# Layer 0's expert products in tiles 32 columns wide, and a written order for the step into layer 1

## The chip, the cores and the metric

The kernel runs as one program on one core of a Trainium2 chip. The metric is the time of one execution on the device in microseconds (us); lower is better. Three runs of the kernel before gave 1434.01, 1437.96 and 1445.67 us, median 1437.96 us. All inputs and outputs are float32.

## The reference, cut to what matters

Two layers work on 256 latent tokens x and 256 context tokens ctx, 1024 features each. Each layer is a mixer, then a mixture of experts. The part of the reference that the change touches is layer 0's mixture and the way into layer 1:

```python
def hier_moe(h, wg, bg, we, be, w1, w3, w2):
    ...                                # top-1 group of 4, top-2 expert in it, weights in combine
    for e in range(16):
        y = (jax.nn.silu(h @ w1[e]) * (h @ w3[e])) @ w2[e]     # 1024 -> 512 -> 1024
        out = out + combine[:, e:e + 1] * y
...
xc = xc + g2_c * y[256:]               # layer 0: context and latent tokens
xl = xl + g2_x * y[:256]
...
hx = modulate(xl, norm_g[1, 0], sh1_x, sc1_x)      # layer 1 begins: RMSNorm, scale, shift
hc = modulate(xc, norm_g[1, 0], sh1_c, sc1_c)
p = hx @ od_w_in, hc @ od_w_in                     # query columns 0:512 are needed of hx alone
```

So layer 1's first projection needs every expert's result for the x tokens, and the same for ctx a little later.

## The kernel before, in words

**Layer 0's experts** (`all0`). Each expert gets up to 96 tokens, gathered by an indirect DMA into `xe` and transposed to `XE` (features on partitions, 96 tokens). The tokens are the stationary operand of TensorE and the weights stream past. 96 does not fit two or four times into 128 columns, so the tokens are cut: 64 of them go into bank A (`h`, slice `ab`), two products side by side (w1 and w3), and 32 into bank C (`hc`, slice `cc`), four products side by side (w1 and w3, two slices of the features each). `hidden(e, q)` does that for a quarter q of the features: four A products, then four C products. In float32 each product is two matmul instructions. `middle(e)` puts A and C together, applies silu and the product (ScalarE, then VectorE), four transposes make `gT`, and `down(e, gT)` multiplies by w2, again 64 tokens wide into `y[0]` and 32 wide into `y[1]`, in two halves of the hidden features. Experts 14 and 15 go through `down` 96 wide instead, and their sums into the tokens are made by TensorE (`last_two`).

The order on an engine is written out where instructions are stamped: `in_line` stamps every matmul and transpose, `put` and `token[0]` stamp ScalarE and VectorE instructions with the name "moe"; stamped instructions of an engine stay in program order. All others are placed by a planner that has its own costs and due times. In loop e the order of TensorE is: hidden(e+1, 0), transposes of gT, hidden(e+1, 1), down(e), transposes of tokens (`xt`), hidden(e+1, 2), transposes, hidden(e+1, 3).

**Weights** come as units of 512 KB through SyncE's DMA queue into a ring of 30 slots, which is cut to 10 after expert 11 (`without(late)`). A slot is filled again when TensorE has used it.

**The step into layer 1.** Experts 0 to 13 write their results to DRAM; 8 indirect DMAs bring them back by token (`room`), and `fetched(n)` adds two of them to 128 tokens: one ScalarE and three VectorE instructions (L940 to L943), n = 0 to 3, the x tokens first. `last_two(a, t)` adds experts 14 and 15: four matmuls into a bank of tag `h` for each half of the features, then two VectorE instructions (L1083, L1084). `norm1_begin` and `norm1_end` norm the x tokens between these. Then `proj1` loads layer 1's first weights (L202), `split` cuts each into a high and a low part (ScalarE `whi`, VectorE `wlo`, both at L224), and `norm1_turn` transposes the x tokens and splits them too. The matmuls of `proj1` (`pj`) also write to banks of tag `h`, of which there are three. None of the weights' splits and transposes here is stamped. The ctx tokens are normed and transposed during the first projection.

Of the kernel before, what the change touches and what calls it, by code (L numbers as in the profile page):

```python
# [135 lines left out]
def tile_kernel(ctx: ExitStack, tc: tile.TileContext, I, out, stage=99, dbg=None):  # L136
# [81 lines left out]
    def flip(*args):  # L218
        inst = nc.tensor.transpose(*args)  # L219
        if in_line[0]:  # L220
            inorder(inst, "line")
# [124 lines left out]
    def norm1_begin(x, t, put):  # L346

        i, n = 1 if t < 2 else 0, token_tile(norm1["xn"], t)
        for h in range(2):
            hs = slice(h * 512, h * 512 + 512)  # L350
            put(act(n[:, hs], token_tile(x, t)[:, hs], AF.Square, accum_out=norm1["st"][:, t, h:h + 1]))
            put(V.tensor_tensor(n[:, hs], token_tile(x, t)[:, hs], norm1["sc"][i][:, hs], op=ALU.mult))

    def norm1_end(t, put):

        i, n, st = 1 if t < 2 else 0, token_tile(norm1["xn"], t), norm1["st"]
        s = st[:, t, 0:1]
        put(V.tensor_tensor(s, s, st[:, t, 1:2], op=ALU.add))
        put(V.tensor_scalar(s, s, 1.0 / D, 1e-6, op0=ALU.mult, op1=ALU.add))
        put(act(s, s, AF.Sqrt))  # L360
        put(V.reciprocal(s, s))
        for g in range(2):
            hs = slice(g * 512, g * 512 + 512)
            put(V.scalar_tensor_tensor(n[:, hs], n[:, hs], s, norm1["sh"][i][:, hs], op0=ALU.mult, op1=ALU.add))

    def norm1_turn(x, khi, klo):

        xn = norm1["xn"]
        xn[0] = cp.tile([P, 2, D], F32, tag="x4", name="xn")
        for t in (2, 3, 0, 1):  # L370
            c = slice(t * 128, t * 128 + 128)
            if t < 2:
                norm1_begin(x, t, lambda inst: None)
                norm1_end(t, lambda inst: None)
            for g in range(2):
                tp = ps("nT", ("ga", "gT")[g])
                for k in range(4):
                    flip(tp[:, k * 128:(k + 1) * 128], token_tile(xn, t)[:, (4 * g + k) * 128:(4 * g + k + 1) * 128],
                         ident)
                split(tp.rearrange("p (k t) -> p k t", k=4), khi[g][:, :, c], klo[g][:, :, c])  # L380
            if t == 3:
                yield xn
        yield

    def split_tiles():

# [63 lines left out]
    def moe(l, tiles, cap, ng, x1, pm, pn, hhi=None, hlo=None):  # L450
# [182 lines left out]
        def experts(pe, ysb, rest, spare=None, next_norm=None):  # L633
# [178 lines left out]
            def all0(rest):  # L812
# [61 lines left out]
                def hidden(e, q):  # L874


                    if q == 0:
                        hs[e] = ps("h", "h"), ps("hc", "h")
                    w = [weights(e, u) for u in (ups[q][1], ups[q][0])]
                    A, C = hs[e]  # L880
                    for i in range(2):
                        for j in range(2):
                            mm(A[64 * j:64 * j + 64, :], XTe[e][:, 2 * q + i, ab], w[j][:, i], start=(q + i == 0),
                               stop=(q + i == 4))
                    for i in range(2):
                        for j in range(2):
                            r0 = 64 * i + 32 * j
                            mm(C[r0:r0 + 32, :], XTe[e][:, 2 * q + i, cc], w[j][:, i], start=(q == 0), stop=(q == 3))
# [22 lines left out]
                def down(e, gT):  # L911


                    y = [ps("y", "y") for _ in range(2)]
                    if e > 13:
                        for f in range(4):
                            w = weights(e, 8 + f)
                            for h in range(2):
                                mm(y[h][r], gT[:, f], w[:, h], start=(f == 0), stop=(f == 3))
                        return y  # L920
                    for g in range(2):
                        ws = [weights(e, 8 + 2 * g + i) for i in range(2)]
                        for i in range(2):
                            for h in range(2):
                                mm(y[0][64 * h:64 * h + 64, :], gT[:, 2 * g + i, ab], ws[i][:, h], start=(g + i == 0),
                                   stop=(g + i == 2))
                        for i in range(2):
                            for h in range(2):
                                r0 = 64 * i + 32 * h
                                mm(y[1][r0:r0 + 32, :], gT[:, 2 * g + i, cc], ws[i][:, h], start=(g == 0), stop=(g == 1))  # L930
                    return y
# [66 lines left out]
                for e in range(16):  # L998
# [9 lines left out]
                    if e < 15:  # L1008
                        hidden(e + 1, 1)
                    else:  # L1010
                        for n in (2, 3):
                            fetched(n, put)
                    y = down(e, gT)
                    if e < 14:
                        o = ysb[:, e % 2, :]
# [48 lines left out]
                                    out=rooms[2 * n_ + i], out_offset=None, in_=yD,  # L1064
                                    in_offset=bass.IndirectOffsetOnAxis(ap=idx[:, i, a:a + 1], axis=0))
                in_line[0] = False
                token[0] = None
                slots[:] = base
                turn[0] = 0
                yhi, ylo, PT = last["yhi"], last["ylo"], last["PT"]  # L1070
                warm(AF.Sqrt, yhi(1, 1)[r])
                sums = pe.tile([P, 2, D], F32, tag="rm0", name="tt")

                def last_two(a, t):

                    for h in range(2):
                        acc = ps("sc", "h")
                        for i in range(2):
                            mm(acc, PT[r, i, a], yhi(i, h)[r], start=(i == 0), stop=False)
                            mm(acc, PT[r, i, a], ylo(i, h)[r], start=False, stop=(i == 1))  # L1080
                        hs_ = slice(h * 512, h * 512 + 512)
                        tt = sums[:, a % 2, hs_]
                        put(V.tensor_tensor(tt, acc, g2[t][:, hs_], op=ALU.mult))  # L1083
                        put(V.tensor_tensor(token_tile(x1, t)[:, hs_], tt, token_tile(x1, t)[:, hs_], op=ALU.add))  # L1084


                begin1, end1 = next_norm[1:]
                last_two(*order[0])
                begin1(x1, 2, put)
                last_two(*order[1])  # L1090
                end1(2, put)
                begin1(x1, 3, put)
                end1(3, put)
                for n in (2, 3):
                    last_two(*order[n])

            def all1():

# [684 lines left out]
    with tc.tile_pool(name="pe0", bufs=1) as pe:  # L1783
        ysb = pP.tile([P, 2, D], F32, tag="vT", name="ysb")

        def spare():
            a = [pe.tile([P, 2, 512], F32R, name=f"yhi{i}") for i in range(2)]
            b = pP.tile([P, 4, 512], F32R, tag="y", name="spare")
            c = pe.tile([P, 2, 512], F32R, name="PT0")
            return (lambda i, h: a[i][:, h]), (lambda i, h: b[:, 2 * i + h]), c.rearrange("p i (a t) -> p i a t", a=4)  # L1790

        experts(pe, ysb, rest, spare, (norm1_scales, norm1_begin, norm1_end))
    es_m.close()
    if "x2" in dbg:
        for i in range(2):
# [31 lines left out]
    with ExitStack() as es:  # L1827
# [1 line left out]
        dqT = xtile([4, 256])  # L1829
        dkT = [xtile([2, 512]) for _ in range(2)]  # L1830
        dv = pP.tile([P, 4, 512], F32, tag="y", name="dv")
        kt = [[pP.tile([P, 4, 512], F32R, tag=t, name=t) for t in tags] for tags in (("rT", "kT"), ("vT", "kkn"))]
        khi, klo = ([t[k // 4][:, k % 4, :] for k in range(8)] for t in kt)
        norm = norm1_turn(x1, *kt)
        with tc.high_priority(offset=150):
            xn = next(norm)
        c1 = pA.tile([P, NC1], F32, name="c1")
        nc.scalar.dma_start(c1, I["cst1"])
        def proj1(c0, n, evac):

            for i in range(4):
                if i % 2 == 0:
                    ws = [wload(Wd[h * 512:(h + 1) * 512, c0 + i * 128:c0 + i * 128 + 256], 4, 256)
                          for h in range(2)]
                whi, wlo = (t.rearrange("p a (k f) -> p (a k) f", f=128) for t in split_tiles())
                for h in range(2):
                    split(ws[h][:, :, (i % 2) * 128:(i % 2 + 1) * 128], whi[:, 4 * h:4 * h + 4, :],
                          wlo[:, 4 * h:4 * h + 4, :])
                acc = ps("pj", "pj")
                for k in range(8):  # L1850
                    mm(acc[:, 0:n], whi[:, k, :], khi[k][:, 512 - n:], start=(k == 0), stop=False)
                    mm(acc[:, 0:n], whi[:, k, :], klo[k][:, 512 - n:], start=False, stop=False)
                    mm(acc[:, 0:n], wlo[:, k, :], khi[k][:, 512 - n:], start=False, stop=(k == 7))
                evac(i, acc)
# [26 lines left out]
        def ev_dq(i, acc):  # L1881
            act(dqT[:, i, :], acc[:, 0:256], AF.Copy)
            rope(dqT[:, i, :])
            if i == 1:
                next(norm)

        def ev_dk(i, acc):
            act(dkT[i // 2][:, i % 2, :], acc, AF.Copy)
# [163 lines left out]
```

## Time and profile before

| | |
|---|---|
| median of three runs | 1437.96 us (1434.01 to 1445.67) |
| the profiled execution | 1443.12 us, its span 1441.1 us |
| mean granted TensorE clock over the span | 0.930 |
| busy: PE, DVE, ACT, POOL | 1267.0, 590.1, 425.6, 218.1 us |
| bytes moved by DMA | 349.22 MB, mean 242 GB/s |

PE is TensorE's matmuls, PEld its weight loads, DVE VectorE, ACT ScalarE, POOL GpSimd, SP SyncE. A matmul's end is modelled, so the distance between starts says more than a duration. Times on the left of a row are us from the start of the span. In brackets stands how long the engine was idle ahead of the row, and what ended that.

### The profile page before, as it was taken

What the parts mean: (1) busy time and instruction counts of PE and PEld (TensorE: products, weight loads), DVE (VectorE), ACT (ScalarE), POOL (GpSimd) and SP (SyncE); (2) the same over time, 40 slices, a digit from 0 to 9 for tenths busy, and PEclk for the clock granted to TensorE, in tenths of its full rate; (3) what the DMA queues carried; (4) which work ended last, traced back from release to release, by engine and by line L of the source; (5) the groups of instructions that cost most, each with busy time, mean ns of one, the idle gap of its engine ahead of it and who ended that gap; (6) DMA issues with size and microseconds to landing.
All of it is one profiled execution on the core that took longest, in us unless ns stands there. A gap on an engine that the chain in (4) does not pass through costs nothing. (4 is left out here: it accounts for less than half of the span.)

```text
span 1441.1 us, 22145 instructions
## 1 busy us (share of the span) xinstructions
PE 1267.0 (88%) x8700; PEld 687.0 (48%) x8700; DVE 590.1 (41%) x1329; ACT 425.6 (30%) x835; POOL 218.1 (15%) x271
## 2 busy tenths in 40 slices
PE   5999778888989886999999987799998699999975
PEld 0556556666756672222222223776766544433321
DVE  1326846778656632222112238744636611110003
ACT  2753322222223321221222123324637321111102
POOL 0005520333411301111111120310000100000000
PEclk9999989989999967999999996799999799999998
DMA  9687677766783757999998790651442679999554
GB/s 335 209 256 216 179 181 203 174 172 177 183 262 129 248 221 275 369 383 383 380 382 304 256 365 23 147 139 59 146 169 88 208 265 398 400 396 395 222 223 172
DMA packets 240320, 349.22 MB, mean 242 GB/s; under 512 B 96120, under 2 KB 126104, under 8 KB 239952
## 3 DMA queue, kind: packets, MB, share of 16 engines
q1 hardware_dynamic: 226240, 304.72, 62.9%
q0 software_dynamic: 11264, 34.72, 7.4%
q10 hardware_dynamic: 2704, 8.27, 1.6%
q8 instruction: 72, 1.18, 0.3%
q14 instruction: 40, 0.33, 0.1%
HBM read 326.86 MB, written 20.79 MB: 241 GB/s over the span
## 5 line engine op out<-in xcount | busy, mean ns | idle before, releaser
L214 PE MATMUL y<-w,gT 128*64 128x512 f32 (+2 forms) x736 | 163.0, 612 | 2.1 <-ACT gT L698 1.5
L214 PE MATMUL pj<-hh,whi 128*128 128x512 f32 x432 | 150.1, 429 | 0.6 <-ACT hh L224 0.3
L214 PE MATMUL h<-w,XT 128*64 128x512 f32 x512 | 138.6, 614 | 5.1 <-issue 5.1
L224 DVE TENSOR_TENSOR wlo<-w,whi 128x512 fp32r<-128x512 f32 (+1 forms) x104 | 84.7, 828 | 111.5 <-ACT whi L224 107.4
L214 PE MATMUL h<-w,XE 128*64 128x512 f32 x512 | 125.4, 611 | 3.0 <-ACT XE L790 2.5
L224 ACT ACTIVATE whi<-w 128x512 fp32r<-128x512 f32 (+1 forms) x104 | 69.9, 700 | 155.4 <-DMA w<-in_ev_w_in_dram 73.0
L214 PEld LDWEIGHTS pj<-hh,whi 128*128 128x128 f32 x432 | 83.6, 202 | 32.4 <-issue 9.8
L214 PEld LDWEIGHTS y<-w,gT 128*64 128x64 f32 (+2 forms) x736 | 44.9, 131 | 101.7 <-issue 91.4
L214 PE MATMUL pj<-hh,wlo 128*128 128x512 f32 x216 | 89.9, 418 | 2.1 <-DVE wlo L224 2.0
L214 PE MATMUL ada<-w,sT 128*32 128x512 f32 x384 | 69.0, 639 | 16.9 <-DMA w<-in_ada_w_dram 10.0
L214 PE MATMUL hc<-w,XE 128*32 128x512 f32 x512 | 68.2, 605 | 0.1
L214 PEld LDWEIGHTS h<-w,XT 128*64 128x64 f32 x512 | 36.4, 138 | 63.6 <-issue 57.6
L894 DVE TENSOR_TENSOR ysb<-y,ysb 64x512 f32<-64x512 f32 x14 | 9.7, 695 | 139.1 <-ACT ysb L893 139.1
L214 PEld LDWEIGHTS h<-w,XE 128*64 128x64 f32 x512 | 31.3, 137 | 57.1 <-issue 48.1
L806 DVE SCALAR_TENSOR_TENSOR ylo<-y,sw,yhi 128x512 fp32r<-128x512 f32 x16 | 12.0, 751 | 100.7 <-ACT yhi L805 100.7
L214 PEld LDWEIGHTS pj<-hh,wlo 128*128 128x128 f32 x216 | 43.5, 201 | 17.0 <-DVE wlo L224 4.7
L689 DVE TENSOR_TENSOR gg<-gg,h 64x512 f32<-64x512 f32 x16 | 11.1, 691 | 95.0 <-ACT gg L688 95.0
L2024 POOL TENSOR_TENSOR x<-x,fg 128x512 f32<-128x512 f32 x2 | 2.8, 1378 | 284.9 <-ACT sq L2023 284.9
L1020 POOL DMA_DIRECT2D yD<-ysb x28 | 15.1, 545 | 171.7 <-ACT ysb L1016 171.7
L1016 ACT ACTIVATE ysb<-y 128x512 f32<-128x512 f32 x14 | 8.4, 597 | 99.6 <-PE y L214 99.6
L1316 DVE TENSOR_TENSOR pr<-T,X 128x8 f32<-128x8 f32 (+14 forms) x120 | 35.7, 298 | 4.0 <-DMA X<-xs 0.6
L893 ACT ACTIVATE gs<-hc 64x512 f32<-64x512 f32 x16 | 9.4, 588 | 88.7 <-PE hc L214 88.7
(542 smaller groups left out, 2269.1 us busy)
## 6 DMA issues: line engine op xcount, KB each, us to landing
w<-in_moe_w_dram SPq DMA_DIRECT2D x384, 512.0 KB
w<-in_ada_w_dram SPq DMA_DIRECT2D x96, 512.0 KB
w<-in_ev_w_in_dram SPq DMA_DIRECT2D x27, 512.0 KB
w<-in_od_w_in_dram SPq DMA_DIRECT2D x24, 512.0 KB
sD<-wad SPq DMA_DIRECT2D x16, 256.0 KB
w<-in_ev_w_out_dram SPq DMA_DIRECT2D x8, 512.0 KB
w<-in_od_w_out_dram SPq DMA_DIRECT2D x8, 512.0 KB
yD<-ysb POOLq DMA_DIRECT2D x28, 128.0 KB, 5.3
```

Source lines behind the costliest of these rows:

```text
L214: inst = nc.tensor.matmul(*args, **kw)
L224: for inst in (act(hi, src, AF.Copy), V.tensor_tensor(lo, src, hi.bitcast(F32), op=ALU.subtract)):
L689: V.tensor_tensor(gg[64:128], gg[64:128], acc[64:128], op=ALU.mult)
L806: V.scalar_tensor_tensor(lo, y, w, hi.bitcast(F32), op0=ALU.mult, op1=ALU.subtract))
L893: put(act(o, acc[0:64, :], AF.Copy))
L894: put(V.tensor_tensor(o, acc[64:128, :], o, op=ALU.add))
L1016: put(act(o[:, 0:512], y[0], AF.Copy))
L1020: nc.gpsimd.dma_start(yD[e * cap:e * cap + 64, hs_], o[64 * h:64 * h + 64, 0:512])
L1316: V.tensor_tensor(pr[:, :, 0:t], T[:, 0:t, :].rearrange("p s j -> p j s"), X[:, 0:t, t][:, None, :].to_broadcast([P, 8, t]), op=ALU.mult)
L2024: (V if h else G).tensor_tensor(xt_[:, hs], xt_[:, hs], fg[:, hs], op=ALU.mult)
```

## The change

Three things. In `hidden` and `down` each product of 64 tokens becomes two of 32 (tokens 0:32 and 32:64), so that all these products have 32 columns and four stand side by side; bank C, `y[1]` and experts 14 and 15 in `down` stay as they were. Layer 1's first two weight loads (columns 0:256) are written in expert 15's loop after gT's copy, and their two splits get a stamped place: the first after `fetched(3)` and ahead of `down(15)`, the second after the x tokens' transposes. The x tokens' transposes and splits are stamped too, each right behind the norm of its 128 tokens, and the ctx sums of `last_two` come last, into banks of the tags `y` and `ps` in place of `h`.

```diff
@@ -363,24 +363,41 @@
             hs = slice(g * 512, g * 512 + 512)
             put(V.scalar_tensor_tensor(n[:, hs], n[:, hs], s, norm1["sh"][i][:, hs], op0=ALU.mult, op1=ALU.add))
 
-    def norm1_turn(x, khi, klo):
-
-        xn = norm1["xn"]
-        xn[0] = cp.tile([P, 2, D], F32, tag="x4", name="xn")
-        for t in (2, 3, 0, 1):
-            c = slice(t * 128, t * 128 + 128)
-            if t < 2:
-                norm1_begin(x, t, lambda inst: None)
-                norm1_end(t, lambda inst: None)
-            for g in range(2):
-                tp = ps("nT", ("ga", "gT")[g])
-                for k in range(4):
-                    flip(tp[:, k * 128:(k + 1) * 128], token_tile(xn, t)[:, (4 * g + k) * 128:(4 * g + k + 1) * 128],
-                         ident)
-                split(tp.rearrange("p (k t) -> p k t", k=4), khi[g][:, :, c], klo[g][:, :, c])
-            if t == 3:
-                yield xn
-        yield
+    def norm1_turn(t):
+
+        if not norm1.get("kt"):
+            norm1["kt"] = [[pP.tile([P, 4, 512], F32R, tag=tg, name=tg) for tg in tags]
+                           for tags in (("rT", "kT"), ("vT", "kkn"))]
+        khi, klo = norm1["kt"]
+        c = slice(t * 128, t * 128 + 128)
+        for g in range(2):
+            tp = ps("nT", ("ga", "gT")[g])
+            for k in range(4):
+                flip(tp[:, k * 128:(k + 1) * 128],
+                     token_tile(norm1["xn"], t)[:, (4 * g + k) * 128:(4 * g + k + 1) * 128], ident)
+            split(tp.rearrange("p (k t) -> p k t", k=4), khi[g][:, :, c], klo[g][:, :, c])
+
+    def norm1_ctx(x):
+
+        norm1["xn"][0] = cp.tile([P, 2, D], F32, tag="x4", name="xn")
+        for t in range(2):
+            norm1_begin(x, t, lambda inst: None)
+            norm1_end(t, lambda inst: None)
+            norm1_turn(t)
+
+    first_w = {}
+
+    def first_weights():
+
+        Wq = I["od_w_in"][0]
+        ws = [wload(Wq[h * 512:(h + 1) * 512, 0:256], 4, 256) for h in range(2)]
+
+        def make(i):
+            whi, wlo = first_w[i] = [t.rearrange("p a (k f) -> p (a k) f", f=128) for t in split_tiles()]
+            for h in range(2):
+                split(ws[h][:, :, i * 128:(i + 1) * 128], whi[:, 4 * h:4 * h + 4, :], wlo[:, 4 * h:4 * h + 4, :])
+
+        return make
 
     def split_tiles():
 
@@ -880,8 +897,9 @@
                     A, C = hs[e]
                     for i in range(2):
                         for j in range(2):
-                            mm(A[64 * j:64 * j + 64, :], XTe[e][:, 2 * q + i, ab], w[j][:, i], start=(q + i == 0),
-                               stop=(q + i == 4))
+                            for b in (0, 32):
+                                mm(A[64 * j + b:64 * j + b + 32, :], XTe[e][:, 2 * q + i, b:b + 32], w[j][:, i],
+                                   start=(q + i == 0), stop=(q + i == 4))
                     for i in range(2):
                         for j in range(2):
                             r0 = 64 * i + 32 * j
@@ -922,8 +940,9 @@
                         ws = [weights(e, 8 + 2 * g + i) for i in range(2)]
                         for i in range(2):
                             for h in range(2):
-                                mm(y[0][64 * h:64 * h + 64, :], gT[:, 2 * g + i, ab], ws[i][:, h], start=(g + i == 0),
-                                   stop=(g + i == 2))
+                                for b in (0, 32):
+                                    mm(y[0][64 * h + b:64 * h + b + 32, :], gT[:, 2 * g + i, b:b + 32], ws[i][:, h],
+                                       start=(g + i == 0), stop=(g + i == 2))
                         for i in range(2):
                             for h in range(2):
                                 r0 = 64 * i + 32 * h
@@ -1008,8 +1027,13 @@
                     if e < 15:
                         hidden(e + 1, 1)
                     else:
+                        load(len(stream))
+                        slots[:] = base
+                        turn[0] = 0
+                        first = next_norm[3]()
                         for n in (2, 3):
                             fetched(n, put)
+                        first(0)
                     y = down(e, gT)
                     if e < 14:
                         o = ysb[:, e % 2, :]
@@ -1064,17 +1088,14 @@
                                     out=rooms[2 * n_ + i], out_offset=None, in_=yD,
                                     in_offset=bass.IndirectOffsetOnAxis(ap=idx[:, i, a:a + 1], axis=0))
                 in_line[0] = False
-                token[0] = None
-                slots[:] = base
-                turn[0] = 0
                 yhi, ylo, PT = last["yhi"], last["ylo"], last["PT"]
                 warm(AF.Sqrt, yhi(1, 1)[r])
                 sums = pe.tile([P, 2, D], F32, tag="rm0", name="tt")
 
-                def last_two(a, t):
+                def last_two(a, t, banks):
 
                     for h in range(2):
-                        acc = ps("sc", "h")
+                        acc = ps("sc", banks[h])
                         for i in range(2):
                             mm(acc, PT[r, i, a], yhi(i, h)[r], start=(i == 0), stop=False)
                             mm(acc, PT[r, i, a], ylo(i, h)[r], start=False, stop=(i == 1))
@@ -1084,15 +1105,19 @@
                         put(V.tensor_tensor(token_tile(x1, t)[:, hs_], tt, token_tile(x1, t)[:, hs_], op=ALU.add))
 
 
-                begin1, end1 = next_norm[1:]
-                last_two(*order[0])
+                begin1, end1, _, turn1 = next_norm[1:]
+                last_two(*order[0], "hh")
                 begin1(x1, 2, put)
-                last_two(*order[1])
+                last_two(*order[1], ("h", "ps"))
                 end1(2, put)
+                turn1(2)
                 begin1(x1, 3, put)
                 end1(3, put)
-                for n in (2, 3):
-                    last_two(*order[n])
+                turn1(3)
+                first(1)
+                last_two(*order[2], "yy")
+                last_two(*order[3], ("ps", "y"))
+                token[0] = None
 
             def all1():
 
@@ -1789,7 +1814,7 @@
             c = pe.tile([P, 2, 512], F32R, name="PT0")
             return (lambda i, h: a[i][:, h]), (lambda i, h: b[:, 2 * i + h]), c.rearrange("p i (a t) -> p i a t", a=4)
 
-        experts(pe, ysb, rest, spare, (norm1_scales, norm1_begin, norm1_end))
+        experts(pe, ysb, rest, spare, (norm1_scales, norm1_begin, norm1_end, first_weights, norm1_turn))
     es_m.close()
     if "x2" in dbg:
         for i in range(2):
@@ -1829,23 +1854,23 @@
         dqT = xtile([4, 256])
         dkT = [xtile([2, 512]) for _ in range(2)]
         dv = pP.tile([P, 4, 512], F32, tag="y", name="dv")
-        kt = [[pP.tile([P, 4, 512], F32R, tag=t, name=t) for t in tags] for tags in (("rT", "kT"), ("vT", "kkn"))]
-        khi, klo = ([t[k // 4][:, k % 4, :] for k in range(8)] for t in kt)
-        norm = norm1_turn(x1, *kt)
-        with tc.high_priority(offset=150):
-            xn = next(norm)
+        khi, klo = ([t[k // 4][:, k % 4, :] for k in range(8)] for t in norm1["kt"])
+        xn = norm1["xn"]
         c1 = pA.tile([P, NC1], F32, name="c1")
         nc.scalar.dma_start(c1, I["cst1"])
         def proj1(c0, n, evac):
 
             for i in range(4):
-                if i % 2 == 0:
+                if i % 2 == 0 and (c0 or i):
                     ws = [wload(Wd[h * 512:(h + 1) * 512, c0 + i * 128:c0 + i * 128 + 256], 4, 256)
                           for h in range(2)]
-                whi, wlo = (t.rearrange("p a (k f) -> p (a k) f", f=128) for t in split_tiles())
-                for h in range(2):
-                    split(ws[h][:, :, (i % 2) * 128:(i % 2 + 1) * 128], whi[:, 4 * h:4 * h + 4, :],
-                          wlo[:, 4 * h:4 * h + 4, :])
+                if c0 or i > 1:
+                    whi, wlo = (t.rearrange("p a (k f) -> p (a k) f", f=128) for t in split_tiles())
+                    for h in range(2):
+                        split(ws[h][:, :, (i % 2) * 128:(i % 2 + 1) * 128], whi[:, 4 * h:4 * h + 4, :],
+                              wlo[:, 4 * h:4 * h + 4, :])
+                else:
+                    whi, wlo = first_w[i]
                 acc = ps("pj", "pj")
                 for k in range(8):
                     mm(acc[:, 0:n], whi[:, k, :], khi[k][:, 512 - n:], start=(k == 0), stop=False)
@@ -1882,7 +1907,7 @@
             act(dqT[:, i, :], acc[:, 0:256], AF.Copy)
             rope(dqT[:, i, :])
             if i == 1:
-                next(norm)
+                norm1_ctx(x1)
 
         def ev_dk(i, acc):
             act(dkT[i // 2][:, i % 2, :], acc, AF.Copy)
```

## Rows read from the trace of the kernel before

**Rows 1.** Stretches: us, busy us of each engine (instructions), granted clock, DMA share, GB/s.
```profile
368.00:376.00 8.00, 8.00 (x124) 5.99 (x123) 2.13 (x11) 0.98 (x2) 5.61 (x5) 1.00 0.58 119
600.00:640.00 40.00, 40.00 (x248) 11.20 (x244) 8.91 (x16) 8.37 (x15) 6.04 (x10) 1.00 1.04 382
867.00:870.00 3.00, 2.14 (x5) 1.18 (x6) 2.77 (x4) 0.63 (x1) 0.00 (x0) 0.50 0.04 11
```

**Rows 2.** Timeline, 640 to 652 us: start, length, engine, line, operation, tiles, count.
```profile
643.80 0.55 PE L219 MATMUL xt<-cst,xe 96*128 96x96 f32 x4
...
646.15 1.07 PE L214 MATMUL hc<-w,XE 128*32 128x512 f32 x8
...
647.14 1.94 PE L214 MATMUL h<-w,XE 128*64 128x512 f32 x8
...
649.01 1.06 PE L214 MATMUL hc<-w,XE 128*32 128x512 f32 x8
...
650.07 0.37 PEld L219 LDWEIGHTS gT<-cst,gg 96*128 96x128 f32 x4 [0.91 <-DVE gg L905]
```

**Rows 3.** Timeline of PE in slivers between 640.9 and 643.7 us, splitting two runs.
```profile
640.94 0.65 PE L214 MATMUL h<-w,XE 128*64 128x512 f32 x2
...
641.42 0.60 PE L214 MATMUL h<-w,XE 128*64 128x512 f32 x2
...
642.27 0.60 PE L214 MATMUL h<-w,XE 128*64 128x512 f32 x2
...
642.80 0.62 PE L214 MATMUL hc<-w,XE 128*32 128x512 f32 x1
...
643.26 0.61 PE L214 MATMUL hc<-w,XE 128*32 128x512 f32 x4
```

**Rows 4.** Timeline of PE, 652.5 to 661 us: `down` of an expert.
```profile
653.42 5.80 PE L214 MATMUL y<-w,gT 128*64 128x512 f32 x32
659.15 0.55 PE L219 MATMUL xt<-cst,xe 96*128 96x96 f32 x4
```

**Rows 5.** DMA issues and groups of PE from the start to 640 us.
```profile
w<-in_moe_w_dram SPq DMA_DIRECT2D x80, 512.0 KB
...
L214 PE MATMUL h<-w,XE 128*64 128x512 f32 x144 | 36.3, 627 | 2.5 <-ACT XE L790 2.5
...
L214 PE MATMUL y<-w,gT 128*64 128x512 f32 x64 | 15.5, 605 | 0.0
```

**Rows 6.** Timeline of all engines, 844 to 901 us: the end of the experts.
```profile
844.79 7.11 PE L214 MATMUL y<-w,gT 128*96 128x512 f32 x16
...
858.77 1.22 DVE L942 TENSOR_TENSOR room<-room,g2t 128x1024 f32<-128x1024 f32 x1
...
864.49 0.63 ACT L224 ACTIVATE whi<-w 128x512 fp32r<-128x512 f32 x1 [4.97 <-DMA w<-in_od_w_in_dram]
865.15 0.69 DVE L224 TENSOR_TENSOR wlo<-w,whi 128x512 fp32r<-128x512 f32 x1 [5.16 <-ACT whi L224]
865.76 1.22 DVE L943 TENSOR_TENSOR x<-room,x 128x1024 f32<-128x1024 f32 x1
...
867.01 0.69 DVE L894 TENSOR_TENSOR gs<-hc,gs 64x512 f32<-64x512 f32 x1
...
867.85 0.77 PE L214 MATMUL sc<-yhi,PT 96*128 96x512 f32 x1 [8.97 <-DVE gs L894]
868.40 0.67 DVE L224 TENSOR_TENSOR wlo<-w,whi 128x512 fp32r<-128x512 f32 x1
...
871.39 10.05 PE L214 MATMUL y<-w,gT 128*96 128x512 f32 x16 [0.58 <-ACT gT L1007]
872.54 1.28 DVE L941 SCALAR_TENSOR_TENSOR room<-room,wk 128x1024 f32<-128x1024 f32 x1 [2.69 <-ACT room L940]
```

**Rows 7.** The same timeline, later: the x tokens' transposes and the first projection.
```profile
891.35 1.92 PE L219 MATMUL nT<-cst,xn 128*128 128x128 f32 x8
...
900.89 0.55 PE L214 MATMUL pj<-rT,whi 128*128 128x256 f32 x1 [0.99 <-DVE tt L1083]
```

## The prediction, made before the changed kernel was run

> **What bounds the kernel now.** I read the page's slices first, then stretches of the expert stage, the timeline of TensorE inside one expert, the ring's lead, and the end of the experts. Between 600 and 640 us TensorE is busy 40.00 of 40 us at full clock, while the 16 DMA engines show a share of 1.04 at 382 GB/s [rows 1]. Two resources look full, so the first question is which one sets the pace. By 640 us SyncE had issued 80 weight units; TensorE had begun 144 A matmuls (8 for 2 units, so 36 units) and 64 wide `y` matmuls (16 for 4 units, 16 units) [rows 5]. 80 less 52 is 28 of 30 slots: the ring is full, and a load waits for TensorE to give a slot back. TensorE sets the pace; the DMA keeps up.
>
> Inside an expert TensorE works in steps: two wide or four narrow products side by side. Wide steps follow each other in 0.43 us (641.42 to 642.27 is two); the first step of a wide run takes 0.48, the change from wide to narrow 0.53, the first narrow step 0.46 [rows 3]; the change from narrow to wide is 646.15 + 0.46 to 647.14, 0.53 [rows 2]. So a change costs 0.10 above a step, and a new run's first load 0.05 (wide) or 0.03 (narrow). A narrow step does as much for 32 tokens in four places as a wide one for 64 in two, so the number of steps stays.
>
> At the end of the experts TensorE stands still for 8.97 us ahead of 867.85 [rows 6]. VectorE had finished L942 of `fetched(1)` at 859.99; next in its queue came not L943 but a split (`wlo`) of layer 1's first weights, for which ScalarE's half waited on a DMA until 864.49 [rows 6]. Expert 15's silu chain (L894) stood behind it.
>
> **The change, part by part.**
>
> *Narrow tiles.* In `hidden` behind transposes (quarters 1, 2, 3) the change goes (0.10), C's first load is hidden (0.03), and A's costs 0.03 in place of 0.05: 0.15 us. From quarter 1 into `down`, and in `down`, four changes go: narrow to wide 0.10 + 0.05, wide to narrow 0.10 + 0.03, twice each: 0.56. As a check, 653.42 to 659.15 [rows 4] is 5.73; twelve steps of 0.43, a first load 0.05, three changes 0.41 and 0.11 to the transposes (643.26 to 643.80 less a step) give 5.73. Quarter 3 into quarter 0 and inside it would save 0.15 + 0.13, but there the cover ends: gT's transposes already wait for VectorE's L905 at 650.07 [rows 2], 3.46 us behind C's last step at 646.61. TensorE alone would be there at 650.01, after the change at 649.73; it waits 0.34 instead of 0.06, and nothing is gained there. Sum: 15 experts x 3 x 0.15 = 6.75, 14 x 0.56 = 7.84, together 14.6 us. I take 14.5.
>
> The uncertain price is the narrow step in a run longer than two, which no run here has. From below it is 0.43 (as many columns stream as in a wide step); the nearest row above is 0.46, the first narrow step. I take 0.43, since the extra of a first step halves with the columns loaded (0.05 to 0.03), so it is the load's own, and later loads lie beside matmuls. At 0.46 for all, 29 of an expert's 36 steps (7 lie under the silu chain) lose 0.87 of 1.01 us, and about 2 us stay.
>
> Instructions rise: a step issues four loads and four matmuls, eight in 0.43 us. In the densest stretch I found, 368 to 376 us, 124 matmuls and 123 loads take 8.00 us [rows 1], 32 ns each, so eight need 0.26 and fit. [...]
>
> An expert takes 18.7 us: gT to `down` 3.35 and `down` 5.73 [rows 2, 4], quarter 2 and quarter 3 like 643.80 to 647.14, 3.34 each, and quarter 0 from there to gT 2.93 [rows 2]. The DMA must then bring an expert's 12 units in 17.7 us. At no higher rate than now it falls back 1 us per expert, 11 us up to expert 11, where the ring is cut anyhow; its lead of 28 units is 28 x 18.7 / 12, about 43 us. So I cost it at nothing.
>
> *The first weights' split.* Without the split in front, L943 (1.22) follows L942 at 859.99 and L894 begins at 861.2. From L894 to expert 15's `down` it was 867.01 to 871.39, of which 0.67 was the split's second half [rows 6]; so `down` starts at 864.9 and not 871.39. Behind it, `fetched(2)` and `fetched(3)` take VectorE from 1.15 us later: 2 x (1.28 + 1.22 + 1.22) = 7.4, to 873.5, and the split, now behind them, two halves of 0.69, to 874.9. [...] Sums of experts 14 and 15 stand ahead of gT in TensorE's queue and wait for banks; I take off 0.5: 6.0 us. [...] The weights had landed by then (first at 864.49), so the stamped place waits for nothing; the two loads are issued in SyncE's queue where they were, behind the experts' last, since that queue waits for slots.
>
> *x tokens' transposes in order, ctx sums last.* The first projection waited 0.99 us for VectorE to read a ctx sum out of a bank of `h` [rows 7]; that goes. Against it, the splits of the first 128 x tokens now stand on ScalarE and VectorE ahead of the second 128's norm, and wait for eight transposes, 1.92 us [rows 7]; before, the norm filled that time. The cost lies between nothing and 1.92 + 0.69 = 2.6 us; I take 1.1, as only the wait from norm to first split stays empty. Together nothing, between +1.0 and -1.6. The ctx sums come no earlier, and the ctx norm behind them neither.
>
> **Sum:** 14.5 + 6.0 = 20.5 us. The profiled execution goes from 1443.12 to 1422.6; it stands 5.2 above the median of 1437.96, from which I forecast 1417.5, say 1418 us.
>
> **The rivals.**
> 1. *The narrow step is 0.46 throughout.* For it: each narrow step in the trace is 0.46, none 0.43. Against: each is the first of its run. 2 + 6 = 8 us: 1430. Chance 0.16.
> 2. *The hole stays.* Another unstamped instruction, the next weights' split or the ctx norm, takes the place in VectorE's or ScalarE's queue, or `down` runs at half clock all through. For it: the planner did so once. Against: what was known to be there now has a stamped place. 14.5 alone: 1423.5. Chance 0.13.
> 3. *The DMA sets the pace from the first expert on.* For it: share 1.04. Against: the full ring. Only the 6.0 remain: 1432. Chance 0.06.
> 4. *Slower: runs of narrow products can't keep stepping*, for instance because the third step's load isn't made beside the second's matmuls, and a step costs as much as a change, 0.53 [rows 3], in place of 0.43. 36 steps lose 3.6 us against 1.01 + 0.34, 2.2 per expert or 31 over 14, and the 6.0 of the end make it +25: 1463. It decides from a step of 0.48 on: 0.05 x 36 = 1.8 is what narrow tiles, the wait at gT and a fourteenth of the 6.0 bring together. For it: no run of more than two narrow steps in the trace. Against: the 32 ns per instruction, and wide runs that keep 0.43. Chance 0.07.
> 5. *The narrow tiles do nothing because the compiled order keeps two side by side*: each run would need twice the steps, far slower than 4; C's four side by side exclude it, and I give it nothing of its own.
>
> **How the numbers follow.** The forecast has 0.58. A measurement of this kernel can tell about 1% from no change, 14.4 us, or 1423.6. Faster by over 1%: nearly all of the forecast (0.55) and half of rival 2 (0.06): 0.61. Slower by over 1%: rival 4's longer steps, 0.05, and 0.02 for what I overlooked: 0.07. The rest is within 1%: 0.32. The forecast's own range is 1411 to 1425: 14.5 with 1 us for the experts' beginning, and 2 to 8 at the end, with the runs' own spread of 4. The range holds rivals 1 to 3 as well: 1409 to 1434.
>
> **What would show it.** `h<-w,XE` 128*32, 1024 matmuls, steps of 0.43 within a run and none of 0.53 before C; `down` from first matmul to the transposes in 5.27 us; gT to gT 17.7 us where it was 18.7; a wait of 0.3 us for L905 at gT. On VectorE L943 directly behind L942, and expert 15's `down` about 3.7 us behind L894. The first `pj` waits for a split of x tokens and not for L1083. It would be wrong if narrow steps show 0.46 or more, if TensorE waits for weights before expert 12, or if TensorE still stands still over 6 us ahead of expert 15's gT.

## The result and the profile after

The changed kernel takes 1420.12 us in the median of four runs (1416.21 to 1423.25), beside 1439.97 us in four runs of the kernel before: a ratio of 0.9851, 95% interval 0.9810 to 0.9892, faster by over 1%. The profiled run took 1416.21 us, 3.9 below its median, with a span of 1414.3 us; the profiled run of before stood 3.2 above its own, so the two traces differ by 26.7 us in the span and the medians by 19.9. Of those 26.7, 1.9 lie behind the first matmul into `pv`, in code that did not change, and 4.0 ahead of expert 0's `gT`, where only that expert's `hidden` did; there the runs that share after's code (e5, e8, e9 below) lie up to 4.5 us apart, so little of the 4.0 can be put down to the change. 20.8 lie between.

First the narrow tiles. The page of after has this group (busy us, mean ns of one; idle before), and its windows have this stretch:

```profile
L214 PE MATMUL h<-w,XE 128*32 128x512 f32 x1024 | 124.5, 604 | 2.5 <-ACT XE L807 2.5
...
600.00:640.00 40.00, 39.71 (x368) 13.05 (x371) 11.75 (x29) 8.90 (x16) 7.02 (x11) 1.00 1.04 382
```

TensorE is nearly as full as in [rows 1], with 368 matmuls where there were 248, and the DMA moves the same 382 GB/s. TensorE's list of waits from 570 to 820 us (waited for: total us, times, longest) holds no DMA; the list of its weight loads, which run beside the matmuls, has nine waits for weights of at most 0.3 us:

```profile
PE gT L219 <- DVE gg L923: 3.5, 11, 0.4
PE PT L219 <- ACT PT L976: 0.6, 1, 0.6
PE hc L214 <- DVE gs L912: 0.4, 1, 0.4
```

One expert in after's timeline of TensorE, answering to [rows 2 to 4]:

```profile
641.83 0.55 PE L219 MATMUL gT<-cst,gg 96*128 96x96 f32 x4 [0.29 <-DVE gg L923]
642.31 1.92 PE L214 MATMUL h<-w,XE 128*32 128x512 f32 x16
644.05 1.04 PE L214 MATMUL hc<-w,XE 128*32 128x512 f32 x8
644.91 5.33 PE L214 MATMUL y<-w,gT 128*32 128x512 f32 x48
650.17 0.55 PE L219 MATMUL xt<-cst,xe 96*128 96x96 f32 x4
...
659.61 0.55 PE L219 MATMUL gT<-cst,gg 96*128 96x96 f32 x4 [0.36 <-DVE gg L923]
```

From start to start, 16 matmuls of A take 1.74 us, four steps of 0.43 with nothing for the change to C; `down` takes 5.26; gT to gT is 17.78 here. Of the thirteen distances from expert 0's `gT` to expert 13's the median is 17.69, against 18.72 before; the means are 17.84 and 18.87, since four distances are longer (18.01 to 18.33). The periods below are such medians.

The end of the experts, VectorE and TensorE of after in order of time, answering to [rows 6, 7]:

```profile
840.52 1.22 DVE L961 TENSOR_TENSOR room<-room,g2t 128x1024 f32<-128x1024 f32 x1
841.78 1.22 DVE L962 TENSOR_TENSOR x<-room,x 128x1024 f32<-128x1024 f32 x1
843.03 0.69 DVE L912 TENSOR_TENSOR gs<-hc,gs 64x512 f32<-64x512 f32 x1
843.78 0.73 PE L214 MATMUL sc<-yhi,PT 96*128 96x512 f32 x1 [3.72 <-DVE gs L912]
847.01 8.92 PE L214 MATMUL y<-w,gT 128*96 128x512 f32 x16 [0.58 <-ACT gT L1026]
...
854.47 1.22 DVE L962 TENSOR_TENSOR x<-room,x 128x1024 f32<-128x1024 f32 x1
855.61 1.29 DVE L224 TENSOR_TENSOR wlo<-w,whi 128x512 fp32r<-128x512 f32 x2
856.81 1.28 DVE L224 TENSOR_TENSOR spare<-y,yhi 96x512 fp32r<-96x512 f32 x2
...
872.67 1.94 PE L219 MATMUL nT<-cst,xn 128*128 128x128 f32 x8 [4.20 <-DVE xn L364]
874.44 0.58 PE L214 MATMUL pj<-rT,whi 128*128 128x256 f32 x1
```

L961 and L962 are the old L942 and L943, L912 the old L894. They now follow each other without a gap; TensorE stands still 3.72 us and not 8.97, and the first projection waits for no ctx sum; its first weight load waits 0.23 us for a split of x tokens (`rT`).

Behind it something came back. The last ctx sum (L1105), the load of the rotary table `c`, the matmul `rp` that needs it and the transposes of the ctx tokens, with GpSimd's addition that runs beside them, and the granted clock (the number behind the five engines' busy times) in the stretches behind the first `pj`:

```profile
883.36 0.69 DVE L1105 TENSOR_TENSOR x<-tt,x 128x512 f32<-128x512 f32 x1
884.08 0.34 ACTq L1860 DMA_DIRECT2D c<-in_cst_dram  x1
890.86 1.26 PE L214 MATMUL rp<-xw,c 128*128 128x256 f32 x4 [3.04 <-DMA c<-in_cst_dram]
890.89 4.50 POOL L1927 TENSOR_TENSOR xn<-xn,c 128x2048 f32<-128x2048 f32 x1 [5.60 <-DMA c<-in_cst_dram]
891.56 0.42 DVE L1902 TENSOR_TENSOR rt__8372<-rp,c 128x256 f32<-128x256 f32 x1 [3.50 <-PE rp L214]
891.90 4.10 DVE L1903 TENSOR_TENSOR xw<-xw,c 128x256 f32<-128x256 f32 x2
897.06 2.11 PE L219 MATMUL nT<-cst,xn 128*128 128x128 f32 x8 [3.44 <-DVE xn L364]
```

```profile
892.00:898.00 6.00, 2.56 (x10) 1.61 (x8) 6.00 (x7) 0.00 (x0) 3.39 (x1) 0.50 0.15 46
898.00:904.00 6.00, 4.60 (x17) 3.66 (x17) 4.65 (x12) 2.19 (x5) 0.00 (x0) 0.50 0.29 89
904.00:912.00 8.00, 6.44 (x30) 5.95 (x29) 6.08 (x11) 1.60 (x3) 5.45 (x8) 0.50 0.45 95
```

TensorE idles for the table and for the ctx norm, and runs 20 us at a granted clock of 0.50 (the three stretches from 892 to 912). The table's buffer is free when the experts' buffers are given back, and those are held by the ctx sums, which the change put last: the last one ends at 884.05, the load is issued at 884.08. Time at the lower clock is not new in this stage, though. From the first `pj` to `pv` the mean granted clock is 0.85 before, 0.83 after and 0.86 in a second profile of after (e5).

The stages of every profiled run, from starts on TensorE, in us (`gT` by expert; `y15` is expert 15's `down`; `pj` and `pv` the first of each, `pv` in `proj_tok`):

| kernel | gT0 to gT13 | gT13 to y15 | y15 to pj | pj to pv | gT0 to pv |
|---|---|---|---|---|---|
| before | 245.4 | 51.4 | 29.5 | 68.9 | 395.2 |
| after | 231.9 | 44.5 | 27.4 | 70.5 | 374.4 |
| after, run again (e5) | 231.9 | 44.5 | 27.4 | 72.5 | 376.4 |
| e1 narrow tiles only | 231.9 | 49.7 | 29.2 | 69.1 | 379.8 |
| e2 order only | 245.4 | 46.1 | 27.4 | 70.1 | 389.1 |
| e3 narrow in `down` only | 237.9 | 50.8 | 28.6 | 69.3 | 386.5 |
| e4 mixed widths | 243.4 | 51.7 | 28.4 | 68.0 | 391.5 |
| e8 weights unstamped | 231.9 | 49.8 | 28.1 | 67.7 | 377.5 |
| e6 table early | 231.9 | 44.1 | 27.4 | 66.4 | 369.9 |
| e7 e6, split later | 231.9 | 44.1 | 27.0 | 68.9 | 371.9 |
| e9 sums in `h` | 231.9 | 43.9 | 32.7 | 64.5 | 373.1 |
| e10 e6, mask later | 231.9 | 46.4 | 27.8 | 67.9 | 374.1 |
| e11 e6, ctx sooner | 231.9 | 44.1 | 27.4 | 65.7 | 369.2 |
| e12 e10 and e11 | 231.9 | 46.2 | 27.6 | 66.3 | 372.1 |

The two profiles of after agree to 0.1 in the first three stages and differ by 2.0 in the fourth, so there a difference of 2 says nothing.

### The profile page after: what moved, and what is told of

It is laid out like the page before. It is cut to its first block, busy times and chain, and to the rows that moved or that the text cites. A ratio compares the mean times of both kernels' runs of the same rounds, so it can differ in the third digit from the quotient of the medians.

```text
span 1414.3 us, 23614 instructions
## 1 busy us (share of the span) xinstructions
PE 1239.4 (88%) x9436; PEld 686.8 (49%) x9436; DVE 592.2 (42%) x1329; ACT 425.5 (30%) x835; POOL 219.0 (15%) x271
## 5 line engine op out<-in xcount | busy, mean ns | idle before, releaser
L214 PE MATMUL y<-w,gT 128*32 128x512 f32 (+2 forms) x960 | 155.3, 600 | 2.4 <-ACT gT L715 1.5
L214 PE MATMUL pj<-hh,whi 128*128 128x512 f32 x432 | 147.2, 422 | 1.0 <-ACT whi L224 0.7
L214 PE MATMUL h<-w,XE 128*32 128x512 f32 x1024 | 124.5, 604 | 2.5 <-ACT XE L807 2.5
L214 PEld LDWEIGHTS y<-w,gT 128*32 128x32 f32 (+2 forms) x960 | 48.5, 120 | 89.3 <-issue 75.1
L214 PE MATMUL ada<-w,sT 128*32 128x512 f32 x384 | 70.5, 659 | 15.0 <-DMA w<-in_ada_w_dram 8.2
L912 DVE TENSOR_TENSOR ysb<-y,ysb 64x512 f32<-64x512 f32 x14 | 9.7, 694 | 128.5 <-ACT ysb L911 128.5
L214 PEld LDWEIGHTS h<-w,XE 128*32 128x32 f32 x1024 | 28.2, 110 | 55.2 <-issue 47.3
L214 PEld LDWEIGHTS pj<-hh,wlo 128*128 128x128 f32 x216 | 42.6, 197 | 17.9 <-DVE wlo L224 5.9
L214 PEld LDWEIGHTS hc<-w,XE 128*32 128x32 f32 x512 | 16.1, 111 | 40.3 <-issue 30.9
```

What stands on the lines that cost most here:

```text
L214: inst = nc.tensor.matmul(*args, **kw)
L912: put(V.tensor_tensor(o, acc[64:128, :], o, op=ALU.add))
```

## The experiments

**Which part brings what.** e1 is before with the loops over `b` in `hidden` and `down`; e2 is after without them.

> The kernel before with the 32-wide tiles in hidden and down, and nothing of the new order. My theory (changes of tile width cost 0.10 us and a first load 0.03 to 0.05, steps are 0.43): gT to gT 17.7 us where before has 18.7, a wait for VectorE at gT, and 14 to 15 us less than before in total, 1425; the stall ahead of expert 15's gT stays near 9 us. Rival (the two halves are not additive, the order brings most of the gain): under 8 us.

> The changed kernel with the wide tiles of before in hidden and down: the order of the step into layer 1 alone. My theory: gT to gT stays 18.7, from expert 14's gT to expert 15's gT 22 to 23 us where before has 28.5, and about 6 us less in total, 1434. Rival (the stall only moves to a later wait): the first projection's start comes 6 us earlier but layer 1's proj_tok (pv) not, and the total is within 2 us of before.

e1: 1427.63 us, ratio 0.9896 (0.9865 to 0.9927). e2: 1437.70 us, 0.9961 (0.9931 to 0.9992). From gT0 to `pv` they gain 15.4 and 6.1 us, 21.5 together, where after gains 20.8 and 18.8. The narrow tiles carry about three quarters, and both rivals are out: e1 gains far more than 8, and of the 7.4 us that e2 wins up to `pj` 6.1 are left at `pv`. In e1 the standstill at expert 15 stays (9.41 us). In e2 the wait for VectorE is gone and expert 15's `down` takes 7.11 us, what expert 14's took in before at a granted clock of 1.00, but TensorE waits for expert 15's last weights instead; from expert 14's gT to expert 15's it is 23.5 us, a little over the 22 to 23 expected:

```profile
855.41 3.37 PE L214 MATMUL h<-w,XE 128*64 128x512 f32 x8 [2.83 <-DMA w<-in_moe_w_dram]
...
863.92 7.11 PE L214 MATMUL y<-w,gT 128*96 128x512 f32 x16 [0.58 <-ACT gT L1024]
```

With both parts it takes 8.92: TensorE arrives sooner at the same VectorE chain, idles 3.72 us and runs the first 3.34 us of `down` at a granted clock of 0.50 (0.97 in the rest).

**Is it the change of width, or the wide product?** e3 is before with narrow tiles in `down` alone; e4 has narrow tiles in `down`, and in `hidden` a mixture that keeps a change of width in every quarter:

```diff
-    mm(A[64 * j:64 * j + 64, :], XTe[e][:, 2 * q + i, ab], w[j][:, i], ...)
+    for b, m in ((0, 32), (32, 32)) if i == 0 else ((0, 64),):
+        mm(A[64 * j + b:64 * j + b + m, :], XTe[e][:, 2 * q + i, b:b + m], w[j][:, i], ...)
```

> The kernel before with 32-wide tiles in down alone; hidden stays 64 and 32. My theory (four changes of width go per expert, 0.56 us): down from its first matmul to the transposes 5.27 us instead of 5.73, gT to gT 18.14. Rival (narrow products as such are quicker): hidden's share can't tell, but then the gain goes with the products, down's 2 of hidden's 4 wide runs, a third of 1.01: 18.36.

> As the run with narrow down, but in hidden the first two A products of a quarter are made 32 wide and the last two 64 wide, so that a quarter has two changes of width (narrow, wide, narrow) where before has one. Same steps, half of A's products narrow. My theory (each change costs 0.10, and a first load): a quarter behind transposes becomes 0.13 us longer than before's, gT to gT about 18.5, slower than with narrow down alone. Rival (narrow products as such are quicker, or their number counts): half of hidden's gain, gT to gT 17.9.

TensorE's timeline of e3, then of e4:

```profile
653.68 0.55 PE L219 MATMUL gT<-cst,gg 96*128 96x96 f32 x4
...
656.91 5.33 PE L214 MATMUL y<-w,gT 128*32 128x512 f32 x48
662.18 0.55 PE L219 MATMUL xt<-cst,xe 96*128 96x96 f32 x4
...
671.82 0.55 PE L219 MATMUL gT<-cst,gg 96*128 96x96 f32 x4
```

```profile
652.35 0.55 PE L219 MATMUL gT<-cst,gg 96*128 96x96 f32 x4
...
661.46 2.07 PE L214 MATMUL h<-w,XE 128*32 128x512 f32 x12
663.47 1.06 PE L214 MATMUL hc<-w,XE 128*32 128x512 f32 x8
...
670.90 0.55 PE L219 MATMUL gT<-cst,gg 96*128 96x96 f32 x4
```

e3's period is 18.14, as the changes counted out of `down` say. e4's is 18.55: half of A's steps were narrow, yet A (661.46 to 663.47) takes 2.01, where after's takes 1.74. The rivals' 18.36 and 17.9 are out: the price sits in the changes. One run each gave 1438.79 and 1442.21 us, beside a median of 1443.93 for before.

**What the split's place is worth in the end.** e8 leaves the first weights' loads and splits to the planner, as before, and keeps the rest of the change; e5 is after once more, e6 and e7 follow.

> The changed kernel itself once more, as the yardstick for the two variants beside it. Every theory: 1.3 to 1.6% under before, gT to gT 17.7 us.

> The changed kernel without its first part of the order: layer 1's first weights are loaded and split in the projection as before, left to the planner; x tokens' transposes and ctx sums keep their stamped order and banks. My theory (the split's place made the stall): a split comes ahead of expert 15's silu chain again and waits for its DMA, from gT of expert 14 to gT of expert 15 is 27 to 28 us, and 5 to 6 us of the gain are lost. Rival (the transposes or the banks removed it): 22 to 23 us as in the changed kernel.

The timeline of e8, ScalarE, VectorE and TensorE:

```profile
843.67 0.63 ACT L224 ACTIVATE whi<-w 128x512 fp32r<-128x512 f32 x1 [4.94 <-DMA w<-in_od_w_in_dram]
844.33 0.69 DVE L224 TENSOR_TENSOR wlo<-w,whi 128x512 fp32r<-128x512 f32 x1 [4.67 <-ACT whi L224]
844.94 1.22 DVE L962 TENSOR_TENSOR x<-room,x 128x1024 f32<-128x1024 f32 x1
...
847.03 0.76 PE L214 MATMUL sc<-yhi,PT 96*128 96x512 f32 x1 [8.47 <-DVE gs L912]
```

The standstill is back, for the reason read from [rows 6]: the split stands ahead of L962 and waits for its weights. The first `pj` comes 6.0 us later behind gT13 (77.9 against 71.9). But e8 is 2.9 and 4.8 us quicker from there to `pv`, and the medians show nothing of it: e8 1421.19 us, 0.9860 (0.9808 to 0.9912); e5 1422.44 us, 0.9854 (0.9814 to 0.9893). Followed from gT13, the changed kernel is ahead of e8 by 6.0 us at `pj`, 4.7 at the end of the last ctx sum (81.5 and 81.4 against 86.2), 2.8 and 2.3 at the matmul `rp`, 3.1 and 1.1 at `pv`.

**Where it is given back.** e6 loads the rotary table into two other buffers (`c1a`, `c1b`) in place of L1860. The loads are written in expert 12's loop; in the trace they are issued at 453.9 and 434.7 us, where the planner put them, ahead of the experts. e7 is e6 with `first(0)` behind the norm of the first 128 x tokens.

```diff
+        c1a = pP.tile([P, 512], F32, tag="gdT", name="c1a")
+        c1b = ada_pool.tile([P, 512], F32, tag="abt", name="c1b")
+        nc.scalar.dma_start(c1a, I["cst1"][:, 0:512])
+        nc.scalar.dma_start(c1b[:, 0:192], I["cst1"][:, 512:704])
...
-        nc.scalar.dma_start(c1, I["cst1"])
```

> The changed kernel with the rotary table (c1) loaded during expert 12 into two buffers that are free by then, in place of a load that can begin only when the experts' pool is given back, behind the last ctx sum. My theory: in the changed kernel the time that the order won ahead of the first projection is partly given back inside it, because the ctx sums stand last and the table's load waits for them (rotary matmul 16.4 us behind the first projection's start, 12.6 before the change); with the table there, the rotary matmul comes within 12 us and layer 1's pv 2 to 5 us sooner, counted from the first projection's start. Rival (the ctx norm's chain sets pv's start, the table is only seen waiting beside it): pv moves by under 1 us.

> As the run with the early table, and the first weights' split (stamped ahead of expert 15's down) moved behind the norm of the first 128 x tokens, where VectorE stands idle 1.18 us for their transposes. My theory: VectorE is late at the split of expert 15's result by about 1 us because this split lies ahead; the first projection starts 0.8 to 1.3 us sooner, counted from the end of expert 15's down. Rival (TensorE's end of down sets it): no change within 0.3 us.

Timeline and windows of e6, whose first `pj` is at 884.8:

```profile
895.83 1.13 PE L214 MATMUL rp<-xw,c1b 128*128 128x256 f32 x4
899.38 4.98 POOL L1931 TENSOR_TENSOR xn<-xn,c1b 128x2048 f32<-128x2048 f32 x1 [3.60 <-DMA xn<-in_relb_dram]
900.46 3.91 DVE L363 TENSOR_TENSOR st<-st 128x1 f32<-128x1 f32 x1
905.42 1.97 PE L219 MATMUL nT<-cst,xn 128*128 128x128 f32 x8 [6.57 <-DVE xn L369]
```

```profile
884.80:902.00 17.20, 13.67 (x85) 12.33 (x84) 15.19 (x28) 9.51 (x23) 8.76 (x10) 0.89 0.76 153
902.00:912.00 10.00, 6.44 (x38) 6.10 (x38) 9.90 (x17) 2.34 (x5) 2.66 (x2) 0.66 0.34 102
912.00:922.50 10.50, 9.52 (x75) 9.12 (x76) 6.75 (x14) 3.89 (x9) 5.18 (x8) 1.00 0.95 194
```

`rp` comes 11.0 us behind `pj` (16.4 in after) and waits for no DMA. The time at a clock of 0.50 is estimated from these rows as twice (1 - clock) times the stretch, as if the clock were either 1.00 or 0.50: 3.8 + 6.8 = 10.6 us, against over 20 in after, and `pv` comes 4.1 and 6.1 us sooner. TensorE's idle time in the stage, its length less the busy time, is hardly less (10.4 us, against 9.7 and 11.8 in after; the wait for the ctx norm is now 6.57): what went is mostly time at the lower clock.

One run's 4 to 6 us stand against 2 between repeats, so I counted in all runs from the end of the last ctx sum, where the late load is issued, to `pv`. The nine runs with the late table take 59.4 to 63.1 us, median 62.3 (before 62.3, after 60.9 and 63.1, e8 59.4), and the five with the early one 55.9 to 59.1, median 56.7. So the late table costs some us; how many is known to no better than the runs' spread. e6's time is 1417.44 us, 0.9832 (0.9786 to 0.9877), 5 us below e5, with intervals that overlap. e7: 1418.42 us, 0.9819 (0.9775 to 0.9863), and its first `pj` came 0.3 to 0.5 us sooner, not the 0.8 and more that I expected; that theory fell.

**Banks of their own and ctx sums last.** e9 is after with all of `last_two` in banks of `h`.

> The changed kernel with all ctx sums of experts 14 and 15 in banks of tag h again, order as in the changed kernel. My theory (the banks are worth about the 0.99 us that the first projection waited before): the first projection starts 0.5 to 2 us later, counted from the end of expert 15's down, since the sums now stand last and hold two of three banks of h. Rival (the planner puts the sums' matmuls behind the first projection's, so no bank is held): within 0.3 us.

```profile
876.57 0.41 PE L214 MATMUL pj<-rT,whi 128*128 128x256 f32 x1
...
879.50 0.34 ACTq L1860 DMA_DIRECT2D c<-in_cst_dram  x1
```

The ctx sums now stand ahead of the first projection, which starts 5.3 us later behind `y15`, more than expected. The table follows 2.9 us behind it (9.6 in after), and from `pj` to `pv` 6.0 and 8.0 us come back: `pv` is no later than in after. 1414.61 us, 0.9826 (0.9790 to 0.9861). Here an earlier first projection by itself buys nothing. The last ctx sum ends 2.1 us sooner behind gT13 than in after, and `pv` comes 1.3 and 3.4 us sooner: it follows the chain of ctx sums, table and ctx norm.

**The ctx norm.** Three variants of e6: e10 moves GpSimd's two mask additions in the text behind the next two projections, e11 calls `norm1_ctx` after the first group of columns (`i == 0` in place of 1), e12 does both.

> As the run with the early table, and GpSimd's two additions of the column mask moved behind the third projection. My theory: while such an addition runs (4.5 us), VectorE's rotary products take 2.0 us in place of 0.4 and TensorE waits 6.6 us for the ctx norm behind them; with the addition away that wait falls to under 4 us, TensorE's clock stays up more of the time, and pv comes 2 to 4 us sooner than in the run with the early table, counted from the first projection's start (66.4 us there). Rival (the ctx norm itself is the chain): the wait stays over 5.5 us and pv moves under 1 us.

> As the run with the early table, with the ctx norm called behind the first quarter of the first projection and not the second. My theory: the planner puts its norm and transposes ahead of the second rotary turn, TensorE's wait for the ctx transposes falls from 6.6 us to 4 to 6. Rival: GpSimd's addition still holds VectorE, and the wait stays within 0.5 us.

> Both of these at once on the early table. My theory: the effects add, TensorE's wait for the ctx transposes is under 3 us, and the kernel is 3 to 8 us under the changed kernel's 1420 in the median. Rival: the time comes back elsewhere, and it is within 2 us of the run with the early table alone.

e10 didn't test its question, and e12 didn't either: the first addition still began 15.1 and 15.0 us behind `pj` (14.6 in e6). e10 took 1420.47 us, 0.9853 (0.9813 to 0.9894). The 2 us more that both take from gT13 to `y15` are an idle stretch of TensorE ahead of expert 14's `down` (2.12 and 1.98 us), whose cause the trace does not name. e11 cut the wait for the ctx norm in two:

```profile
890.85 0.66 PE L219 MATMUL nT<-cst,xn 128*128 128x128 f32 x4 [1.72 <-DVE xn L369]
895.80 1.12 PE L219 MATMUL nT<-cst,xn 128*128 128x128 f32 x4 [4.28 <-DVE st L364]
```

6.00 us remain of 6.57, at the edge of both the theory and its rival, and `pv` is 0.7 sooner than in e6. 1415.19 us, 0.9834 (0.9794 to 0.9873). e12 waits the same 5.99 and not under 3, so its theory fell; 1416.05 us, 0.9826 (0.9791 to 0.9861). e6, e7, e9, e11 and e12 all have medians of 1414.6 to 1418.4, below after's 1420.1 and 1422.4; no interval stands clear of after's, so a kernel that beats it is likely but not shown.

## Why the prediction was right, point by point

**Sum.** 20.5 us were forecast; the medians give 19.9, the traces from gT0 to `pv` 20.8 and 18.8. 1420 lies in the forecast's own range.

**Narrow tiles: right.** Forecast 17.7 a period, `down` 5.27, a wait of 0.3 at `gT`; measured 17.69, 5.26 and, for the two `gT` shown, 0.29 and 0.36. The taken price, 0.43 for a narrow step in a long run, holds, so rivals 1 and 4 are out. e1 alone gains 15.4 against 14.5. e4 pays for each change (its A takes 2.01, after's 1.74); the rows give the price, 0.10 a change. The eight instructions of a narrow step fit into 0.43, as the forecast took from the 32 ns each of [rows 1].

**DMA at no cost: right.** TensorE's matmuls wait for no weights from 570 to 820 us, at 382 GB/s from 600 to 640; rival 3 is out.

**The first weights' split: right up to the first projection, then mis-sized.** Forecast 6.0 there: the 6.5 by which `down` was to start sooner, less 0.5 for waits for banks. No run shows the 0.5 by itself; e8 against after shows 6.0. L943 came directly behind L942 as described, VectorE was late next, and `down` began 3.98 behind L894, 3.7 forecast; it took 8.92 at a mean granted clock of 0.79, between the 7.11 and the 10.05 of before's experts 14 and 15 [rows 6], whose clocks were 1.00 and 0.70. The failed step is that what comes sooner at `pj` comes sooner at the end: only 3.1 or 1.1 us are left at `pv`. VectorE's work around expert 15's `down` was not the last thing late. The ctx sums end inside the first projection, 4.7 us sooner and not 6.0, and the table's load and the ctx norm begin behind them; from there to `pv` after and its repeat need 1.5 and 3.7 us more than e8, which lies within the spread of the nine runs with a late table. That an early table would save the whole 6.0 is not shown, since no run has it with the split in its old place.

**x turn and ctx sums: net nothing, not told apart from it, and for a part not foreseen.** The forecast looked at the bank of `h`, worth 1, and at ScalarE and VectorE. e8, which keeps this part, is 0.9 us ahead of e1 at `pj` and 2.3 at `pv`, about the repeat's 2. The forecast said that the ctx sums come no earlier, but not that the rotary table's load waits for them. Both parts of the order together bring 5.4 and 3.4 us (after against e1) and 6.1 with wide tiles (e2), close to the forecast's 6.0. As the split alone brought less than its 6.0, a part of that closeness is luck; how much, the repeat's 2 us leave open. Rival 2, the hole staying, is out as a whole (3.72 is left of 8.97), though TensorE still waits there for the same VectorE chain.

## What to carry to other kernels

Count changes of tile width on TensorE like instructions: where it is the bound, products of one width side by side saved 0.10 us a change here, though they need more instructions. When a stall is taken away, follow the time to the last stage that shares a buffer with it: here 6 us were won ahead of a projection, and about half or more was gone at its end. That end follows work inside the projection, which came only 4.7 us sooner, and a DMA that waits for that work's buffers. Time won at one place is to be counted at the end of the chain, and from the right start: from the first projection's start the runs scatter by 8 us, and from the end of the last ctx sum those with an early and a late table no longer overlap. An engine that has become quicker can meet the old chain sooner and pay with idle time and a lower clock, as expert 15's `down` does (8.92 us at a mean granted clock of 0.79, 7.11 us in e2).

## Of the hardware, not expected

Some of VectorE's instructions took far longer than elsewhere while GpSimd added 128x2048 elements: of two L1903, 0.41 us each elsewhere, the first took 3.77 beside L1927 (4.50; the row above shows both, 4.10), and in e6 an L363 on 128x1, 0.15 us elsewhere, took 3.91 beside L1931 (4.98). L1902, which reads the matmul result `rp`, took its usual 0.42 in after's stretch. Why it differs from them, no row shows. The price for the whole kernel is open, since e10 and e12 did not move the addition away.
